# Experts in a written-out order on three engines: second product between the halves of the activation, slot work ahead, no weight splits on GpSimd

## Chip, cores, metric

One core of a Trainium2 chip runs the whole program. The metric is the device time of one execution in microseconds, as the median of several runs.

## What is computed

Two blocks act on 512 tokens of width 1024 in fp32. The first is a mixer (attention over selected keys beside a state-space branch), then a mixture of 32 experts with four experts a token; the second block is a gated mixer and a recurrent one. The change lies in the experts. Cut to them, the reference does this for every block of rows that one expert serves:

```python
def run_block(args):
    toks, e = args
    xb = h_pad[toks]
    gu = xb @ w_gu[e] + b_gu[e]
    g, u = gu[:, :D_EXPERT], gu[:, D_EXPERT:]
    g = jnp.minimum(g, SWIGLU_LIMIT)
    u = jnp.clip(u, -SWIGLU_LIMIT, SWIGLU_LIMIT)
    act = (u + 1.0) * (g * jax.nn.sigmoid(SWIGLU_ALPHA * g))
    return act @ w_dn[e] + b_dn[e]
...
out = out.reshape(n_rows, D) * row_gate[:, None].astype(out.dtype)
y = jax.ops.segment_sum(out, row_tok, num_segments=T + 1)[:T]
```

w_gu has 1024 x 2048 and w_dn 1024 x 1024 numbers an expert, 12 MiB together.

## The kernel before

The experts are ranked by how many tokens chose them. The first 17 ranks (NBIG) are *big*: they take up to 128 rows and compute in three matmuls of halves. A weight piece of 128 x 2048 numbers, 1 MiB, is *split* (split, L351) in two blocks of 1024 columns: ScalarE casts a block to H (L363), VectorE subtracts it from the raw piece and writes the rest to L (L365), and mm3 (L382 to L384) does the row halves against H, L and H. There are four H and four L buffers. The other 15 ranks are *small*: up to 64 rows, and the matmuls take the raw piece as it is.

The weights come by SP's queue in pieces of 1 MiB (wraw, L1690) into eleven buffers that are used in turn: eight pieces of w_gu and four of w_dn an expert. A load waits until the piece that had its buffer has been read: by the split for a big expert, by PE for a small one.

moe (from L1717 on) goes through the experts in the order TURNS. turns (L35) makes that list: three big ones first, then small and big in strict alternation, a small one last. In each turn it traces, in this order: the first product with w_gu (up, L1555, 96 matmuls and 4 for the bias; up64, L1571, 64 and 4); beside its pieces, one step a piece, the generator following, which fetches the expert after the next (one-hot L1542, slot product L1526 on PE, five or six small VectorE operations, gather on GpSimd's queue L1476); the transposes of the next expert's rows (transposed L1488, turned64 L1511); the first piece of the expert before's w_dn; the activation (glu, L1583); the rest of the expert before's second product (down L1629 and L382 to L384, 48 matmuls; down64 L1600 and L1606); the transposes of the activation (acted L1619, turned L1501). The scaled result goes out by a scatter that adds (L1645).

Traced order is not issue order. A scheduler sets each engine's order by priorities and readiness, and so a later product's matmuls can stand between two transposes. The second product that a turn traces is always that of the expert before.

glu (L1583 to L1593), for 512 columns at a time:

```python
nc.vector.tensor_scalar(g, gb, 7.0, None, op0=OP.min)
nc.scalar.activation(s, g, AF.Sigmoid, scale=1.702)
nc.vector.tensor_scalar(u, ub, 7.0, -7.0, op0=OP.min, op1=OP.max)
nc.gpsimd.tensor_tensor(s, s, g, op=OP.mult)
nc.vector.scalar_tensor_tensor(u, u, 1.0, s, op0=OP.add, op1=OP.mult)
```

A big expert runs it twice, a small one once. In a big expert's first product, GpSimd makes the first L block of pieces 1, 3 and 5 (pool=(1, 3, 5)), but not for the first expert in TURNS: 48 blocks.

inorder (L303) is there already and can chain VectorE's instructions in traced order; the expert stage does not use it.

Of the kernel before, what the change touches and what calls it, by code (L numbers as in the profile page):

```python
# [15 lines left out]
OP = mybir.AluOpType  # L16
AX = mybir.AxisListType

P = 128
D = 1024  # L20
S = 512
NT = 4
KD = 8
NE = 32
# [6 lines left out]
NBIG = 17  # L31
# [3 lines left out]
def turns():  # L35
    lead = max(1, 2 * NBIG - NE + 1)
    out, big = list(range(lead)), list(range(lead, NBIG))
    for r in range(NBIG, NE):
        out += [r] + big[:1]
        big = big[1:]  # L40
    return out
# [220 lines left out]
class Kern:  # L262
# [36 lines left out]
    @contextmanager  # L299
    def inorder(self, on=True):  # L300

        traced = self.nc.cur_bb.bb.instructions
        start = len(traced)  # L303
        yield
        last = None
        for i in traced[start:] if on else ():
            if i.engine == mybir.EngineType.DVE:
                if last is not None:
                    self.tc.add_manual_dep(i, last.name, mybir.DependencyInfo(mybir.DependencyClass.NoSync, mybir.DependencyReason.DATA), reason="in order")
                last = i  # L310

# [1206 lines left out]

    def slots(self, dst, oh, meta):

        nc = self.nc
        s0, n = dst
        b = self.bank()
        for e in range(n):
            for t in range(NT):
                nc.tensor.matmul(b[:, 4 * e:4 * e + 4], lhsT=oh[e][:, t], rhs=meta[:, t, s0 + e], start=t == 0, stop=t == NT - 1)  # L1526
        ms = self.small([P, n, 4])
        nc.vector.tensor_copy(ms, b[:, :4 * n].rearrange("p (e k) -> p e k", e=n))
        return self.slot_row(ms, n), ms
# [14 lines left out]

    def slot(self, r, oh, small=False):

        u, ms = self.slots((r, 1), [oh], self.meta)
# [36 lines left out]
    def glu(self, gb, ub):  # L1584

        nc = self.nc
        g, u, s = self.w2(), self.w2(), self.w2()
        nc.vector.tensor_scalar(g, gb, 7.0, None, op0=OP.min)  # L1588
        nc.scalar.activation(s, g, AF.Sigmoid, scale=1.702)  # L1589
        nc.vector.tensor_scalar(u, ub, 7.0, -7.0, op0=OP.min, op1=OP.max)  # L1590
        nc.gpsimd.tensor_tensor(s, s, g, op=OP.mult)  # L1591
        nc.vector.scalar_tensor_tensor(u, u, 1.0, s, op0=OP.add, op1=OP.mult)
        return u  # L1593

    def down64(self, x, sel, ws, gate, last=False):
# [11 lines left out]
        o = self.w4(shape=(P, 512)) if last else self.w2()  # L1607
        nc.vector.scalar_tensor_tensor(o, b, gate, self.gf2, op0=OP.mult, op1=OP.mult)
        return o

# [13 lines left out]
    def down(self, hl, sel, ws, gate, gf):  # L1624
# [11 lines left out]
        o = self.w4()  # L1636
        for n in range(2):
            sl = slice(n * 512, (n + 1) * 512)
            nc.vector.scalar_tensor_tensor(o[:, sl], bs[n], gate, gf[:, sl], op0=OP.mult, op1=OP.mult)
        return o  # L1640

# [86 lines left out]
    def moe(self):  # L1728
# [13 lines left out]
        def fetch(i):  # L1742

            r = TURNS[i]
# [5 lines left out]
            out[i] = self.gather(self.gidx[:64 if r >= NBIG else P, r:r + 1])  # L1750

        def following(i):
            if i == 0:
                self.route()
                yield
                self.slot(0, oh)
                fetch(1)
# [15 lines left out]
        prev = []  # L1773
        for i, r in enumerate(TURNS):
            small = r >= NBIG
            wg, wd = weights(i)
            if i:
                sel = (self.select64 if small else self.select)(self.eid[:, r:r + 1])
            self.bg = [following(i)]
            if small:  # L1780
                bs = self.up64(hl, sel, wg)
            else:
                with ExitStack() if i else self.tc.issue_after(self.first.ins):
                    bs = self.up(hl, sel, [(k, 0, lambda k=k: self.wraw(wg(k)), 2 * D) for k in range(KD)], (1, 3, 5) if i else ())
            if i == 0:
                self.rowload(self.gf, self.mrow[3], nc.gpsimd)
                for h in range(2):
                    row = self.mrow[3]
                    nc.gpsimd.dma_start(self.gf2[64 * h:64 * h + 64], bass.AP(tensor=row.tensor, offset=row.offset + 512 * h, ap=[[0, 64], [1, 512]]))
            self.drain()  # L1790
            if i + 1 < NE:
                hl = (self.turned64 if TURNS[i + 1] >= NBIG else self.transposed)(out.pop(i + 1))
            for step in prev[:1]:
                step()
            us = [self.glu(*bs)] if small else [self.glu(bs[n], bs[2 + n]) for n in range(2)]
            for step in prev[1:]:
                step()
            ah = self.turned(us[0]) if small else self.acted(us)

            def steps(r=r, small=small, ah=ah, sel=sel, wd=wd):  # L1800

                gate = self.gate[:, r:r + 1]
                got = {}

                def piece(kk):
                    if kk not in got:
                        w = self.wraw(wd(kk))
                        got[kk] = w if small else self.split(w)
                    return got.pop(kk)

                def begin():
                    got[0] = piece(0)

                def end():
                    o = self.down64(ah, sel, piece, gate, r == TURNS[-1]) if small else self.down(ah, sel, piece, gate, self.gf)
                    if r == TURNS[-1]:
                        return o
                    self.scatter(o, (self.sidx if small else self.gidx)[:, r:r + 1], small)
                return begin, end
            prev = steps()  # L1820
        o = prev[1]()
        row = self.t([P, 2048], "raw", 4)
# [32 lines left out]
    def overflow(self, gf):  # L1855
# [4 lines left out]
        with tc.For_i(0, n, 1) as i:  # L1860
# [49 lines left out]
            for t in range(NT):  # L1910
                nc.vector.tensor_scalar(oh[:, t], self.mcc("iota128"), col[:, t:t + 1], None, op0=OP.is_equal)
            u, ms = self.slots((0, 1), [oh], meta)
            gate = self.pt([P, 1], "ovg")
# [12 lines left out]
            bs = self.up(hl, sel, [(k, 0, lambda k=k: piece(wg[k * P:(k + 1) * P]), 2 * D) for k in range(KD)])  # L1926
            ah = self.acted([self.glu(bs[n], bs[2 + n]) for n in range(2)])
            o = self.down(ah, sel, lambda kk: self.split(piece(wd[kk * 256:(kk + 1) * 256].rearrange("(p k) n -> p (k n)", k=2))), gate, gf)
            for t, bs in enumerate(self.combine(u, o)):
# [367 lines left out]
```

## Time and profile before

| | |
|---|---|
| median of 3 runs | 2448.7 us (2447.04 to 2450.4) |
| the profiled execution's own time | 2447.35 us |
| its span, first to last instruction | 2445.6 us |
| mean granted clock of TensorE | 0.969 |
| PE busy | 2236.2 us (91%) |
| PE weight loads | 1591.1 us (65%) |
| VectorE | 1527.0 us (62%) |
| ScalarE | 988.5 us (40%) |
| GpSimd | 510.7 us (21%) |
| moved by DMA | 576.38 MB, mean 236 GB/s |

Busy times are shares of the whole span, over stages with different limits. Matmuls overlap, and PE counts as busy until the modelled end of one. A row of a timeline gives the start, the length, the line, the operation, out<-in, and in brackets how long the engine stood idle before it and what it waited for. at and mm are the two sets of four PSUM banks, H and L the split weights, hl the split rows, raw and XU the weight buffers, sx a small expert's turned rows.

### The profile page before, as it was taken

What the parts mean: (1) busy time and instruction counts of PE and PEld (TensorE: products, weight loads), DVE (VectorE), ACT (ScalarE), POOL (GpSimd) and SP (SyncE); (2) the same over time, 40 slices, a digit from 0 to 9 for tenths busy, and PEclk for the clock granted to TensorE, in tenths of its full rate; (3) what the DMA queues carried; (4) which work ended last, traced back from release to release, by engine and by line L of the source; (5) the groups of instructions that cost most, each with busy time, mean ns of one, the idle gap of its engine ahead of it and who ended that gap; (6) DMA issues with size and microseconds to landing.
All of it is one profiled execution on the core that took longest, in us unless ns stands there. A gap on an engine that the chain in (4) does not pass through costs nothing. (4 is left out here: it accounts for less than half of the span.)

```text
span 2445.6 us, 28109 instructions
## 1 busy us (share of the span) xinstructions
PE 2236.2 (91%) x10217; PEld 1591.1 (65%) x10217; DVE 1527.0 (62%) x2374; ACT 988.5 (40%) x1371; POOL 510.7 (21%) x274
## 2 busy tenths in 40 slices
PE   6999999998899889998889898889959999999898
PEld 4676666776776555565555565555537888888676
DVE  7778778765897555666655666655552443538864
ACT  4434443332664333344433344433323422326651
POOL 2011103322233222222222222221210111101210
PEclk9999999999999999999999999999979999999999
DMA  7233253644889999999999999999742222213220
GB/s 296 94 104 126 90 198 140 240 157 167 358 337 378 360 370 372 356 347 374 364 363 381 353 346 364 369 360 363 299 170 86 86 90 94 92 61 112 86 86 35
DMA packets 93940, 576.38 MB, mean 236 GB/s; under 512 B 12591, under 2 KB 14361, under 8 KB 32611
## 3 DMA queue, kind: packets, MB, share of 16 engines
q1 hardware_dynamic: 79856, 540.60, 58.1%
q0 software_dynamic: 8432, 18.21, 3.3%
q10 hardware_dynamic: 5508, 15.71, 1.8%
q8 instruction: 82, 1.34, 0.2%
q14 instruction: 62, 0.51, 0.1%
HBM read 556.74 MB, written 27.59 MB: 239 GB/s over the span
## 5 line engine op out<-in xcount | busy, mean ns | idle before, releaser
L365 DVE TENSOR_TENSOR L<-raw,H 128x1024 fp32r<-128x1024 f32 x439 | 613.4, 1430 | 264.5 <-ACT H L363 263.5
L363 ACT CAST H<-raw 128x1024 fp32r<-128x1024 f32 x501 | 515.8, 1048 | 410.0 <-PE mm L384 189.6
L365 POOL TENSOR_TENSOR L<-raw,H 128x1024 fp32r<-128x1024 f32 x62 | 167.6, 2705 | 514.7 <-ACT H L363 514.6
L383 PE MATMUL mm<-L,hl 128*128 128x512 f32 x544 | 217.4, 400 | 40.5 <-POOL L L365 23.1
L384 PE MATMUL mm<-H,hl 128*128 128x512 f32 x544 | 213.5, 393 | 0.0
L382 PE MATMUL mm<-U,H 128*128 128x512 f32 (+1 forms) x488 | 187.8, 385 | 3.0 <-DVE U L703 3.0
L383 PE MATMUL mm<-U,H 128*128 128x512 f32 (+1 forms) x488 | 186.8, 383 | 0.0
L384 PE MATMUL mm<-U,L 128*128 128x512 f32 (+1 forms) x488 | 186.0, 382 | 0.0
L1580 PE MATMUL mm<-raw,sx 128*64 128x512 f32 x792 | 177.5, 598 | 0.0
L382 PE MATMUL mm<-E,H 128*128 128x512 f32 x416 | 173.5, 419 | 3.7 <-ACT E L388 3.7
L382 PE MATMUL mm<-H,U 128*128 128x512 f32 x424 | 170.0, 401 | 2.6 <-DVE XU L2118 1.2
L382 PE MATMUL mm<-H,hl 128*128 128x512 f32 x544 | 170.4, 393 | 0.6 <-ACT hl L388 0.6
L383 PE MATMUL mm<-L,U 128*128 128x512 f32 x424 | 168.7, 398 | 0.0
L384 PE MATMUL mm<-H,U 128*128 128x512 f32 x424 | 168.4, 398 | 0.0
L383 PE MATMUL mm<-E,H 128*128 128x512 f32 x416 | 166.9, 401 | 1.5 <-DVE E L389 1.4
L384 PE MATMUL mm<-E,L 128*128 128x512 f32 x416 | 166.3, 400 | 0.0
L383 PEld LDWEIGHTS mm<-L,hl 128*128 128x128 f32 x544 | 102.1, 188 | 77.3 <-POOL L L365 30.2
L1591 POOL TENSOR_TENSOR w<-w,w 128x512 f32<-128x512 f32 x49 | 70.3, 1434 | 355.3 <-ACT w L1589 355.3
L1588 DVE TENSOR_SCALAR w<-mm 128x512 f32<-128x512 f32 x49 | 33.7, 687 | 171.8 <-PE mm L1580 152.2
L1589 ACT ACTIVATE w<-w 128x512 f32<-128x512 f32 x49 | 30.9, 631 | 262.5 <-DVE w L1588 262.4
L1580 PEld LDWEIGHTS mm<-raw,sx 128*64 128x64 f32 x792 | 54.9, 137 | 105.9 <-issue 102.8
L383 PE MATMUL at<-L,hl 128*128 128x512 f32 x272 | 118.6, 436 | 1.0 <-DVE L L365 1.0
(444 smaller groups left out, 4060.1 us busy)
## 6 DMA issues: line engine op xcount, KB each, us to landing
raw<-in_w_gu_dram SPq DMA_DIRECT2D x212, 1024.0 KB
raw<-in_w_dn_dram SPq DMA_DIRECT2D x103, 1024.0 KB
XU<-in_w_gu_dram SPq DMA_DIRECT2D x44, 1024.0 KB
XU<-in_w_dn_dram SPq DMA_DIRECT2D x25, 1024.0 KB
raw<-in_win_dram SPq DMA_DIRECT2D x20, 1024.0 KB
raw<-in_w_ada_dram SPq DMA_DIRECT2D x16, 1024.0 KB
raw<-in_wug_dram SPq DMA_DIRECT2D x16, 1024.0 KB
raw<-in_wxg_dram SPq DMA_DIRECT2D x12, 1024.0 KB
```

The lines of the kernel that those rows point to most:

```text
L363: nc.scalar.copy(h[:, :m], src)
L365: eng.tensor_tensor(l[:, :m], src, h[:, :m].bitcast(F32), op=OP.subtract)
L382: t.matmul(out, lhsT=lhs[0], rhs=rhs[0], start=start, stop=False)
L383: t.matmul(out, lhsT=lhs[0], rhs=rhs[1], start=False, stop=False)
L384: t.matmul(out, lhsT=lhs[1], rhs=rhs[0], start=False, stop=stop)
L1580: nc.tensor.matmul(bs[i // 2][64 * (i % 2):64 * (i % 2) + 64], lhsT=x[:, k], rhs=w[:, i * 512:(i + 1) * 512], start=False, stop=k == KD - 1)
L1588: nc.vector.tensor_scalar(g, gb, 7.0, None, op0=OP.min)
L1589: nc.scalar.activation(s, g, AF.Sigmoid, scale=1.702)
L1591: nc.gpsimd.tensor_tensor(s, s, g, op=OP.mult)
```

## The change

- TURNS: the first expert is big, then small and big alternate, and the 16 big ones are spread evenly over the 14 gaps between small ones, so that two gaps hold two.
- inorder takes a set of engines and keeps its last instruction over calls; from the second turn on, the instructions of PE, VectorE and ScalarE are chained in traced order.
- glu, down and down64 end early and hand back a function for their last VectorE operations. The turn calls them at set places: the activation's end (then) behind the split of the third w_dn piece of a big expert's second product, or ahead of a small one's; the second product's own end and its scatter (settle) behind the first split of the next big expert's first product, or ahead of a small expert's.
- A big expert's first two w_dn pieces (one in a big turn) are split ahead of the activation of the turn (begin).
- The selection matrix of the next expert is made at the end of a turn.
- fetch is a generator: one-hot, two steps later the slot product, a step later the slot's operations and the gather; in a small expert's turn the two next experts are fetched.
- GpSimd makes no weight split and no multiplication of the activation: pool=() and nc.vector in glu.

```diff
 def turns():
+    big, small = list(range(1, NBIG)), list(range(NBIG, NE))
+    gaps = max(1, len(small) - 1)
...
+    def inorder(self, on=True, engines=(mybir.EngineType.DVE,), last=None):
...
-    def up(self, hl, sel, pieces, pool=(1, 3, 5)):
+    def up(self, hl, sel, pieces, pool=(), then=None):
...
             w = self.split(w(), n, pool=k in pool)
+            if then and k == pieces[0][0]:
+                then()
...
-        nc.gpsimd.tensor_tensor(s, s, g, op=OP.mult)
-        nc.vector.scalar_tensor_tensor(u, u, 1.0, s, op0=OP.add, op1=OP.mult)
-        return u
+        def end():
+            nc.vector.tensor_tensor(s, s, g, op=OP.mult)
+            nc.vector.scalar_tensor_tensor(u, u, 1.0, s, op0=OP.add, op1=OP.mult)
+            return u
+        return end
...
             oh = self.w2(F32R, (P, NT, P))
             self.onehot(r, oh, small=r >= NBIG)
-            u = self.slot(r, oh, r >= NBIG)
+            yield
+            yield
+            b = self.counted([oh], self.meta, r, 1)
+            yield
+            u = self.slot(r, b, r >= NBIG)
...
-            if i + 2 < NE:
-                yield
-                fetch(i + 2)
-                yield
+            yield from fetch(i + 2)
+            if TURNS[i] >= NBIG:
+                yield from fetch(i + 3)
...
+                def ws(kk):
+                    w = d.got.pop(kk) if kk in d.got else d.piece(kk)
+                    if kk == 2 and not d.small:
+                        then()
+                    return w
...
+            with self.inorder(i > 0, (ET.PE, ET.DVE, ET.Activation), order):
+                if small:
+                    settle()
+                    bs = self.up64(hl, sel, wg)
+                else:
+                    with ExitStack() if i else self.tc.issue_after(self.first.ins):
+                        bs = self.up(hl, sel, [(k, 0, lambda k=k: self.wraw(wg(k)), 2 * D) for k in range(KD)], then=settle)
...
+                self.drain()
+                if down:
+                    down.begin(0 if down.small else 2 if small else 1)
+                glus = [self.glu(*bs)] if small else [self.glu(bs[n], bs[2 + n]) for n in range(2)]
+                if i + 1 < NE:
+                    hl = (self.turned64 if TURNS[i + 1] >= NBIG else self.transposed)(out.pop(i + 1))
+                us = []
+                then = lambda: us.extend(g() for g in glus)
+                if down:
+                    down.products(then)
+                    due.append(down.end)
+                else:
+                    then()
+                osel = sel
+                if i + 1 < NE:
+                    sel = selected(i + 1)
+                    if TURNS[i + 1] >= NBIG:
+                        settle()
+                ah = self.turned(us[0]) if small else self.acted(us)
+                down = Down(r, ah, osel, wd)
```

The overflow loop, which serves experts with more rows than they can hold, calls the split functions one after the other and computes as before.

How the instructions stand now is shown at two places. The first is PE at the end of a small expert's first product (the last L1580 rows; L1501 turns the small expert's activation, the L382 to L384 rows on at are the second product of the big expert before, L1526 a slot product). Before:

```order
L1580 MATMUL mm_7442<-raw_1667_7502,sx_7357 64x512 x2
L1580 MATMUL mm_7441<-raw_1668_7508,sx_7357 64x512 x2
L1580 MATMUL mm_7442<-raw_1668_7508,sx_7357 64x512 x2
L1501 MATMUL at_7636<-cst_66,w_1678_7540 128x128 x4
L382 MATMUL at_7547<-H_7531,hl_7416 128x512
L382 MATMUL at_7548<-H_7531,hl_7416 128x512
L1526 MATMUL at_7703<-meta_4966,w_1715_7701 128x4 x4
L383 MATMUL at_7547<-L_7532,hl_7416 128x512
L384 MATMUL at_7547<-H_7531,hl_7416 128x512
```

Now (line numbers have moved: L1590 is the first product, L1493 the transposes of the next expert's rows, L1645 and L387 to L389 the second product of the big expert before):

```order
L1590 MATMUL mm_8080<-raw_1814_8165,sx_8008 64x512 x2
L1590 MATMUL mm_8081<-raw_1814_8165,sx_8008 64x512 x2
L1493 MATMUL at_8198<-cst_66,w_1700_7663 128x128 x4
L1493 MATMUL at_8205<-cst_66,w_1700_7663 128x128 x4
L1645 MATMUL at_8212<-bias_4818,sel_7788 128x512
L1645 MATMUL at_8213<-bias_4818,sel_7788 128x512
L387 MATMUL at_8212<-H_8173,hl_8056 128x512
L388 MATMUL at_8212<-L_8174,hl_8056 128x512
L389 MATMUL at_8212<-H_8173,hl_8056 128x512
```

The activation's transposes, which stood right behind the first product, have given their place to the next expert's transposes and the second product; no slot product stands there.

The second place is the start of the next big expert's first product (its matmuls write mm). PE before:

```order
L384 MATMUL at_7547<-H_7613,hl_7416 128x512
L383 MATMUL at_7548<-L_7614,hl_7416 128x512
L384 MATMUL at_7548<-H_7613,hl_7416 128x512
L382 MATMUL mm_7653<-H_7659,hl_7514 128x512
L382 MATMUL mm_7654<-H_7659,hl_7514 128x512
L382 MATMUL mm_7655<-H_1708_7663,hl_7514 128x512
L382 MATMUL mm_7656<-H_1708_7663,hl_7514 128x512
```

And now:

```order
L387 MATMUL at_8213<-H_8270,hl_8056 128x512
L388 MATMUL at_8213<-L_8271,hl_8056 128x512
L389 MATMUL at_8213<-H_8270,hl_8056 128x512
L1506 MATMUL at_8289<-cst_66,w_1826_8192 128x128 x4
L387 MATMUL mm_8304<-H_8310,hl_8197 128x512
L388 MATMUL mm_8304<-L_8311,hl_8197 128x512
L389 MATMUL mm_8304<-H_8310,hl_8197 128x512
L387 MATMUL mm_8305<-H_8310,hl_8197 128x512
```

The four transposes of the small expert's activation (L1506) now stand between the last matmul of the second product and the first of the next big expert. ScalarE at the same place, where H_7659 and H_8310 are the first casts of the big expert; before:

```order
L1589 ACTIVATE w_1679_7541<-w_1677_7539 128x512
L363 CAST H_7531<-raw_1672_7529 128x1024
L363 CAST H_1675_7535<-raw_1672_7529 128x1024
L1502 COPY sx_7635<-at_7636 128x512
L363 CAST H_7565<-raw_1682_7563 128x1024
L363 CAST H_7569<-raw_1682_7563 128x1024
L1512 COPY sx_7855<-at_7856 128x512
L363 CAST H_7587<-raw_1687_7585 128x1024
L363 CAST H_1690_7591<-raw_1687_7585 128x1024
L363 CAST H_7609<-raw_7607 128x1024
L363 CAST H_7613<-raw_7607 128x1024
L363 CAST H_7659<-raw_7657 128x1024
```

Now:

```order
L368 CAST H_8183<-raw_8181 128x1024
L368 CAST H_8187<-raw_8181 128x1024
L1599 ACTIVATE w_1827_8193<-w_1825_8191 128x512
L393 CAST hl_8197<-at_8198 128x512
L393 CAST hl_8197<-at_8205 128x512
L368 CAST H_8242<-raw_8240 128x1024
L368 CAST H_1836_8246<-raw_8240 128x1024
L368 CAST H_8266<-raw_8264 128x1024
L368 CAST H_8270<-raw_8264 128x1024
L1507 COPY sx_8288<-at_8289 128x512
L368 CAST H_8310<-XU_8308 128x1024
```

The copy of the turned activation (sx, L1502 before, L1507 now) has moved from behind the second product's first two casts to behind its last, right ahead of the first cast of the big expert; two casts of w_dn now stand ahead of the sigmoid (the ACTIVATE row), where the sigmoid stood ahead of the first.

## Rows read from the trace of the kernel before

**Rows 1.** Windows: PE, PEld, DVE, ACT, POOL busy us (count), granted clock, DMA share, GB/s.

```profile
640.00:1760.00 1120.00, 1012.70 (x4512) 643.79 (x4510) 706.57 (x829) 479.34 (x535) 305.23 (x158) 0.97 0.96 363
820.00:830.00 10.00, 6.66 (x28) 4.71 (x25) 7.81 (x13) 4.99 (x6) 3.57 (x2) 0.83 1.01 425
1110.00:1130.00 20.00, 16.66 (x75) 12.72 (x72) 13.48 (x20) 12.86 (x15) 3.58 (x2) 0.91 1.01 418
```

**Rows 2.** Waits of weight loads (PEld) for a DMA, 640 to 1780: us, times, longest.

```profile
PEld at L1606 <- DMA raw<-in_w_gu_dram: 6.6, 20, 0.4
...
PEld mm L1580 <- DMA raw<-in_w_dn_dram: 2.8, 11, 0.3
```

**Rows 3.** Waits of PE from 640 to 1780 us: sum, times, longest.

```profile
PE at L1501 <- DVE w L1592: 45.7, 14, 3.3
PE mm L383 <- POOL L L365: 23.1, 16, 1.6
PE at L1526 <- DVE w L1542: 18.9, 13, 1.5
PE mm L383 <- DVE L L365: 17.2, 14, 1.3
```

**Rows 4.** Timeline of PE: start us, us, what; openings of three small experts.

```profile
1016.85 1.17 PE L1576 MATMUL mm<-bias,selz 128*128 128x512 f32 x4
...
1090.42 1.17 PE L1576 MATMUL mm<-bias,selz 128*128 128x512 f32 x4
...
1234.62 1.17 PE L1576 MATMUL mm<-bias,selz 128*128 128x512 f32 x4
```

**Rows 5.** Timeline of VectorE and GpSimd behind a small expert's first product.

```profile
1036.75 0.69 DVE L1588 TENSOR_SCALAR w<-mm 128x512 f32<-128x512 f32 x1 [10.06 <-PE mm L1580]
...
1038.24 1.78 POOL L1591 TENSOR_TENSOR w<-w,w 128x512 f32<-128x512 f32 x1 [14.20 <-ACT w L1589]
...
1040.06 0.69 DVE L1592 SCALAR_TENSOR_TENSOR w<-w,w 128x512 f32<-128x512 f32 x1 [1.16 <-POOL w L1591]
```

**Rows 6.** Timeline of PE behind the same product.

```profile
1040.90 1.09 PE L1501 MATMUL at<-cst,w 128*128 128x128 f32 x4 [3.34 <-DVE w L1592]
...
1043.92 0.63 PE L384 MATMUL at<-H,hl 128*128 128x512 f32 x1
1044.35 0.63 PE L383 MATMUL at<-L,hl 128*128 128x512 f32 x1
...
1049.49 0.39 PE L383 MATMUL at<-L,hl 128*128 128x512 f32 x1
1049.72 0.39 PE L384 MATMUL at<-H,hl 128*128 128x512 f32 x1
```

**Rows 7.** Window behind that hole (columns as in rows 1).

```profile
1040.90:1047.70 6.80, 6.80 (x20) 5.70 (x21) 5.07 (x9) 2.47 (x3) 1.79 (x1) 0.50 1.01 419
```

**Rows 8.** Low halves (L365): ns min/median/max, first and last; one stretch of VectorE.

```profile
L365 DVE TENSOR_TENSOR L<-raw,H x279: 1205/1218/4130, 640.8 to 1730.1; 128x1024 fp32r<-128x1024 f32 x140
L365 POOL TENSOR_TENSOR L<-raw,H x39: 2371/2931/3375, 661.4 to 1717.1; 128x1024 fp32r<-128x1024 f32 x39
...
1060.65 6.21 DVE L365 TENSOR_TENSOR L<-XU,H 128x1024 fp32r<-128x1024 f32 x3
```

**Rows 9.** Timeline of PE at a big expert's start.

```profile
1059.65 0.50 PE L383 MATMUL mm<-L,hl 128*128 128x512 f32 x1 [1.26 <-DVE L L365]
...
1063.55 0.50 PE L383 MATMUL mm<-L,hl 128*128 128x512 f32 x1 [1.57 <-POOL L L365]
```

**Rows 10.** ScalarE's copy of the turned activation and its casts: ns min/median/max.

```profile
L1502 ACT COPY sx<-at x14: 585/585/590, 763.9 to 1692.8; 128x512 f32<-128x512 f32 x14
...
L363 ACT CAST H<-raw x318: 1027/1049/1061, 640.3 to 1759.1; 128x1024 fp32r<-128x1024 f32 x159
```

**Rows 11.** DMA: the software queue's share of the span; the gathers' us to landing.

```profile
q0 software_dynamic: 8432, 18.21, 3.3%
...
w<-hd,gidx POOLq DMA_INDIRECT x31, 9.2
```

More of the change, by code (lines that the diff above doesn't have):

```diff
@@ L35, in turns @@
 def turns():
[L36 to L40, printed above, removed]
+    big, small = list(range(1, NBIG)), list(range(NBIG, NE))
+    gaps = max(1, len(small) - 1)
+    upto = lambda k: (2 * k * len(big) + gaps) // (2 * gaps)
+    more = [upto(k + 1) - upto(k) for k in range(gaps)]
+    out = [0]
+    for k, r in enumerate(small):
+        out.append(r)
+        if k < gaps:
+            out, big = out + big[:more[k]], big[more[k]:]
     return out
@@ L304, in inorder @@
         yield
-        last = None
+        last = {} if last is None else last
         for i in traced[start:] if on else ():
[L307 to L310, printed above, removed]
+            if i.engine in engines:
+                if i.engine in last:
+                    self.tc.add_manual_dep(i, last[i.engine].name, mybir.DependencyInfo(mybir.DependencyClass.NoSync, mybir.DependencyReason.DATA), reason="in order")
+                last[i.engine] = i
     def early(self, dt=F32, shape=(P, 4, 512)):
@@ L1543, in onehot, with slot @@
                                             pos[:, :, r:r + 1].to_broadcast([P, NT, P]), op=OP.is_equal)
-    def slot(self, r, oh, small=False):
-        u, ms = self.slots((r, 1), [oh], self.meta)
+    def slot(self, r, b, small=False):
+        u, ms = self.slots(b, 1)
         nc = self.nc
@@ L1606, in down64, with end @@
                     nc.tensor.matmul(b[64 * i:64 * i + 64], lhsT=x[:, j, 64 * h:64 * h + 64], rhs=w[:, k % 2 * D + i * 512:k % 2 * D + (i + 1) * 512], start=False, stop=k == KD - 1)
-        o = self.w4(shape=(P, 512)) if last else self.w2()
-        nc.vector.scalar_tensor_tensor(o, b, gate, self.gf2, op0=OP.mult, op1=OP.mult)
-        return o
+        def end():
+            o = self.w4(shape=(P, 512)) if last else self.w2()
+            nc.vector.scalar_tensor_tensor(o, b, gate, self.gf2, op0=OP.mult, op1=OP.mult)
+            return o
+        return end
     def acted(self, us):
@@ L1635, in down, with end @@
                     self.mm3(bs[n], (hl[:, 0, k * P:(k + 1) * P], hl[:, 1, k * P:(k + 1) * P]), w(j * D + n * 512, 512), False, k == KD - 1)
[L1636 to L1640, printed above, removed]
+        def end():
+            o = self.w4()
+            for n in range(2):
+                sl = slice(n * 512, (n + 1) * 512)
+                nc.vector.scalar_tensor_tensor(o[:, sl], bs[n], gate, gf[:, sl], op0=OP.mult, op1=OP.mult)
+            return o
+        return end
     def scatter(self, o, tok, small=False):
@@ L1742, in fetch @@
         def fetch(i):
+            if i >= NE or i in fetched:
+                return
+            fetched.add(i)
             r = TURNS[i]
@@ L1750, in fetch @@
             out[i] = self.gather(self.gidx[:64 if r >= NBIG else P, r:r + 1])
+        fetched = {0}
         def following(i):
@@ L1755, in following @@
                 yield
[L1756 to L1757 removed]
+                self.slot(0, self.counted([oh], self.meta, 0, 1))
+                yield from fetch(1)
                 yield
[L1759 to L1762 removed]
+            yield from fetch(i + 2)
+            if TURNS[i] >= NBIG:
+                yield from fetch(i + 3)
         def weights(i):
@@ L1771, in weights, with selected, __init__, piece @@
             return lambda k: g[k * P:(k + 1) * P], lambda kk: d[kk * 256:(kk + 1) * 256].rearrange("(p k) n -> p (k n)", k=2)
-        self.bg = []
-        prev = []
+        def selected(i):
+            r = TURNS[i]
+            return (self.select64 if r >= NBIG else self.select)(self.eid[:, r:r + 1])
+        class Down:
+            def __init__(d, r, ah, sel, wd):
+                d.r, d.ah, d.sel, d.wd, d.small, d.got = r, ah, sel, wd, r >= NBIG, {}
+            def piece(d, kk):
+                w = self.wraw(d.wd(kk))
+                return w if d.small else self.split(w)
+            def begin(d, n):
+                for kk in range(n):
+                    d.got[kk] = d.piece(kk)
+            def products(d, then):
+                gate = self.gate[:, d.r:d.r + 1]
+                def ws(kk):
[3 more added lines that the diff above has]
+                    return w
+                if d.small:
+                    then()
+                    d.finish = self.down64(d.ah, d.sel, ws, gate, d.r == TURNS[-1])
+                else:
+                    d.finish = self.down(d.ah, d.sel, ws, gate, self.gf)
+            def end(d):
+                self.scatter(d.finish(), (self.sidx if d.small else self.gidx)[:, d.r:d.r + 1], d.small)
+        self.bg = []
+        down, due, order = None, [], {}
+        ET = mybir.EngineType
+        def settle():
+            while due:
+                due.pop(0)()
         for i, r in enumerate(TURNS):
@@ L1776, in moe @@
             wg, wd = weights(i)
-            if i:
-                sel = (self.select64 if small else self.select)(self.eid[:, r:r + 1])
             self.bg = [following(i)]
[L1780 to L1819, printed above, removed]
@@ L1820, in moe @@
-            prev = steps()
-        o = prev[1]()
+            with self.inorder(i > 0, (ET.PE, ET.DVE, ET.Activation), order):
[5 more added lines that the diff above has]
+                        bs = self.up(hl, sel, [(k, 0, lambda k=k: self.wraw(wg(k)), 2 * D) for k in range(KD)], then=settle)
+                if i == 0:
+                    self.rowload(self.gf, self.mrow[3], nc.gpsimd)
+                    for h in range(2):
+                        row = self.mrow[3]
+                        nc.gpsimd.dma_start(self.gf2[64 * h:64 * h + 64], bass.AP(tensor=row.tensor, offset=row.offset + 512 * h, ap=[[0, 64], [1, 512]]))
+                self.drain()
[9 more added lines that the diff above has]
+                    due.append(down.end)
+                else:
+                    then()
+                osel = sel
[5 more added lines that the diff above has]
+                down = Down(r, ah, osel, wd)
@@ L1822, in moe @@
+        settle()
+        down.products(lambda: None)
+        o = down.finish()
         row = self.t([P, 2048], "raw", 4)
@@ L1926, in overflow @@
             bs = self.up(hl, sel, [(k, 0, lambda k=k: piece(wg[k * P:(k + 1) * P]), 2 * D) for k in range(KD)])
-            ah = self.acted([self.glu(bs[n], bs[2 + n]) for n in range(2)])
-            o = self.down(ah, sel, lambda kk: self.split(piece(wd[kk * 256:(kk + 1) * 256].rearrange("(p k) n -> p (k n)", k=2))), gate, gf)
+            ah = self.acted([self.glu(bs[n], bs[2 + n])() for n in range(2)])
+            o = self.down(ah, sel, lambda kk: self.split(piece(wd[kk * 256:(kk + 1) * 256].rearrange("(p k) n -> p (k n)", k=2))), gate, gf)()
             for t, bs in enumerate(self.combine(u, o)):
```

10 lines of the change are left out of this document (5 added, 5 removed).

## Prediction

> **What bounds the kernel now.** I read the views in this order: busy time by stretch, waits, one interval in order of time, the lengths of single operations. The page's slices put the DMA's full load into one stage, the experts, from 640 to 1760 us. There PE is busy 1012.7 of 1120 us, and the DMA is busy 96% of the time at 363 GB/s [rows 1]. So two candidates stand close together, and the reader has to see which of them ends the waits. PE hardly ever waits for a load: the two largest sums of weight loads held up by a DMA are 6.6 and 2.8 us, in pieces of at most 0.4 us [rows 2]. What PE waits for is computed [rows 3]: 14 times 3.3 us for the activation's product (45.7 us), 13 times 1.45 us for the one-hot of a slot (18.9 us), 23.1 and 17.2 us for low halves of a weight split. The loads for their part wait for buffers that these consumers hold. The stage is paced by PE and its chains, with the DMA not far behind.
>
> The pace is regular. The bias products that open a small expert start at 1016.85, 1090.42 and 1234.62 us [rows 4]: one interval of 73.6 us, then two of 72.1, mean 72.6. An interval holds one big and one small expert. Its largest hole follows the small expert's first product: clamp, sigmoid, GpSimd's multiplication of 1.78 us and a last VectorE operation come one after another [rows 5], and PE stands still for 3.34 us [rows 6]. [...] A stretch of 6.8 us at half speed loses 3.4 us, one of half that length 1.7; the 73.6 us interval holds the longer, the 72.1 us ones by their difference of 1.5 us the shorter, so the mean loss is 2.3 us.
>
> **The change part by part.** (a) The second product of the expert before now stands on PE right behind a small expert's first product, and the activation's end runs beside its third quarter. The 48 matmuls last 48 x 0.23 = 11.0 us; the chain that they hide lasted about 4 us. Saved: 3.3 us an interval, plus the clock's 2.3. If this cover went (the second product itself not ready), the 3.3 us would be back.
>
> (b) One-hots are made two pieces ahead of the four slot products, and both slots of a pair are fetched while a small expert runs. Saved: 1.45 us an interval. The slot work only moves within VectorE; it leaves the big expert's first product, where VectorE has the most to do.
>
> (c) The 48 weight splits and the activation's multiplications leave GpSimd. VectorE's split takes 1.218 us at the median, but up to 4.13 us; three beside a GpSimd split (2.93 us) took 6.21 us, 2.07 each [rows 8]. VectorE thus gets 48 x 1.22 = 59 us more splits and 49 multiplications, at the 0.69 us of its like operation [rows 5] 34 us. Against that stands its own contention: GpSimd's 48 splits take 48 x 2.93 = 141 us, at 2.07 a piece 68 of VectorE's run beside them and lose 0.85 each, 58 us. Net 35 us more, on an engine that is idle for 413 of 1120 us [rows 1]: I count nothing, and that idle time is the cover. In a big expert's first product VectorE then needs 16 x 1.22 = 19.5 us and 1.4 us for finishing the product before, PE 100 x 0.23 = 23 us: PE stays ahead as the slower. With every split at 2.07 us it would be 33 us; that is the upper bound of this part, and it lacks the GpSimd split that makes the 2.07.
>
> (d) What is late next is the start of a big expert's first product. Before, its first casts could run ahead of it; PE had 1.26 and 1.57 us of waiting there [rows 9], 40.3 us in all with 14 to 16 of each [rows 3], 2.8 an interval. Now ScalarE, in written order, makes the copy of the small expert's turned activation first. That copy needs four transposes that stand on PE behind the whole second product. Then come the cast and the low half: about 0.2 for the transposes' end, 0.59 and 1.05 [rows 10], 1.8 us until the first matmul, 1.22 - 0.23 = 1.0 until the second, and about 1.0 more when the two operations that finish the product before (0.7 us each) push back the third low half. New wait 3.9 us, 1.1 more than now. Whether the clock falls behind it no row shows: 1.26 and 1.57 with nine matmuls between them left it at 1.0, 3.34 in one piece did not. 2.9 us with one matmul in it lies nearer to the latter; I take half of 2.3, 1.2 us, between bounds of 0 and 2.3.
>
> (e) The order of experts: three big ones led, then strict alternation; now big and small alternate from the second on, and two pairs of big ones lie inside. The same 17 and 15 experts: nothing, give or take 5 us. In the first turn the second expert's gather is issued behind the fifth of eight pieces instead of the second; three pieces of 12 matmuls are left, 8.3 us, and a gather lands in 9.2 [rows 11]: a miss of 1 us or 2, once, inside those 5. SP's loads keep their order, weight blocks one after the other, and none passes another.
>
> **Sum.** 72.6 - 3.3 - 1.45 - 2.3 + 1.1 + 1.2 = 67.8 us, so 4.8 saved in each of 14 turns with a wait: 67 us. The DMA must still fit: an interval loads 24 MiB, 25.2 MB; stretches of 10 and 20 us run at 425 and 418 GB/s [rows 1], which makes 60 us. The software queue's gathers and scatters had 3.3% of the span [rows 11], 81 us for 32 experts, 5 an interval. 65 us fit into 67.8, but with little to spare, and eleven buffers, at 2.5 us a load, even out only 28 us; I take 10 us off for loads that come late. The gain is 57 us. The profiled execution took 2447.35 us, 1.3 under the median of 2448.7, so I forecast **2390 us**. With no more wait in (d) than before and no half-speed stretch, an interval takes 65.5 us, which the DMA's 65 just allow: 14 x 7.1 = 99, less the same 10, gives the low bound 2358. With the full 2.3 us of clock in (d), 5 us in (e) and 15 for late loads it is 14 x 3.7 - 20 = 32: 2415.
>
> [...]
>
> **The rivals.** *The DMA keeps its busy time.* If the 96% are true work, and the slow packets of the partly idle stretches stay slow when the loads come faster, only the 4% idle can go: 0.04 x 1120 = 45 us at best, half of it likely, 2425 us. For it: the mean of 363 against 418. Against it: the high rates appear just where several loads are queued, the low ones where each waits for a buffer.
>
> *No change.* The loads cannot do better than 363 GB/s on average, whatever PE does: 2447 us. [...] Against it stand the 20 us at 418.
>
> *Slower: written order behind a late load.* ScalarE and VectorE now make the splits of the next second product's first two pieces ahead of a small expert's clamp and sigmoid. If those pieces have not landed, the activation waits with them, and so does PE. Before, the sigmoid went first. Two pieces late are 2 x 2.5 us, then 2.3 us of cast and low half, and a half-speed stretch of 2.3: 9.6 us an interval. It decides from 4.8 us on, two loads late. I price it at 7 us, 2 above the gain: 14 x 2 = 28 us, 2475 us. For it: a small expert's first product takes 8 MiB in 15 us, faster than any rate above. Against it: today's loads are late by 0.4 us at most [rows 2], and eleven buffers run ahead.
>
> **How the numbers follow.** The forecast (2358 to 2415) has 0.62, the DMA that keeps its busy time (2402 to 2447) 0.20, no change 0.06, slower 0.12. A measurement tells about 0.2%, 4.9 us, from no change. Faster by more: 0.62 and nearly all of 0.20, 0.81. Within: 0.06 and the edge of the second case, 0.08. Slower: 0.11. The range that leaves out no more than 2 in 10 is 2358 to 2450.
>
> **What would show it.** Right: no PE wait behind the activation's last operation in the list of waits; none for a one-hot; every VectorE split near 1.22 us; intervals near 67 to 68 us; a new wait of 2 and 1 us at the big expert's first matmuls behind the turned copy; DMA rate above 380 GB/s over the stage. Wrong: intervals of 70 us with PE waiting for loads of weights (the DMA), unchanged intervals, or a sigmoid that starts late behind a cast that waited for a load.

## Result, and the profile after

The changed kernel takes 2369.18 us (median of 4 runs, 2367.14 to 2374.91) against 2449.55 us for the kernel before: a ratio of 0.9676, with an interval of 0.9657 to 0.9696. The profiled execution took 2369.02 us, 78.3 less than that of before; 57 were forecast.

| | before | after |
|---|---|---|
| span | 2445.6 us | 2366.8 us |
| PE busy | 2236.2 us | 2224.0 us |
| VectorE | 1527.0 us | 1523.1 us |
| GpSimd | 510.7 us | 309.1 us |
| mean granted clock | 0.969 | 0.972 |

No engine lost much busy time but GpSimd, which was never the busiest (PE lost 12 us). What went is idle time in the expert stage. Its windows answer to [rows 1]; the second is one interval (columns as there):

```profile
640.00:1690.00 1050.00, 1005.38 (x4522) 648.36 (x4523) 707.82 (x932) 479.10 (x539) 104.49 (x61) 0.98 0.98 388
1101.80:1168.10 66.30, 63.92 (x291) 40.60 (x290) 43.67 (x59) 29.27 (x33) 6.71 (x5) 0.97 0.99 395
```

The DMA moved 363 GB/s before, and moves 388 now, 395 in the interval. The openings of three small experts answer to [rows 4] (timeline of PE):

```profile
1033.06 1.17 PE L1586 MATMUL mm<-bias,selz 128*128 128x512 f32 x4
...
1100.65 1.17 PE L1586 MATMUL mm<-bias,selz 128*128 128x512 f32 x4
...
1232.59 1.17 PE L1586 MATMUL mm<-bias,selz 128*128 128x512 f32 x4
```

One interval of 67.6 us, then two of 66.0, mean 66.5: 6.1 less than before. The waits of PE over the stage answer to [rows 3]:

```profile
PE mm L387 <- ACT H L368: 25.9, 16, 1.6
PE mm L388 <- DVE L L370: 14.3, 20, 0.8
...
PE at L1516 <- DMA w<-hd,gidx: 2.0, 1, 2.0
```

The activation's 45.7 us, the one-hot's 18.9 and GpSimd's 23.1 are gone. In their place stands the wait that the prediction named, for the big expert's first cast (16 times 1.62 us) and its low half (16 times 0.76 us; the other four of the 20 are 0.53 us at its third low half). One gather was late, once, by 2.0 us. The same place in order of time, PE first and then ScalarE, answers to [rows 9, 10]:

```profile
1062.01 0.63 PE L1506 MATMUL at<-cst,w 128*128 128x128 f32 x4
1064.25 0.49 PE L387 MATMUL mm<-H,hl 128*128 128x512 f32 x1 [1.62 <-ACT H L368]
1065.51 0.80 PE L388 MATMUL mm<-L,hl 128*128 128x512 f32 x1 [0.76 <-DVE L L370]
...
1066.53 0.63 PE L387 MATMUL mm<-H,hl 128*128 128x512 f32 x1
1066.96 0.63 PE L388 MATMUL mm<-L,hl 128*128 128x512 f32 x1
```

```profile
1062.67 0.58 ACT L1507 COPY sx<-at 128x512 f32<-128x512 f32 x1 [5.01 <-PE at L1506]
1063.15 3.88 ACT L368 CAST H<-XU 128x1024 fp32r<-128x1024 f32 x4
```

The chain reads as forecast: transposes (L1506), the copy (sx), the cast (H), PE's first matmul after 1.62 us, its second 0.76 us later. Behind it matmuls start 0.43 us apart: the granted clock is 0.50 from 1066 to 1070 us. The half speed follows in 12 of the 16 starts. In the other four the same two waits leave the clock at 1.00, and there the third low half is waited for as well:

```profile
822.84 0.49 PE L387 MATMUL mm<-H,hl 128*128 128x512 f32 x1 [1.62 <-ACT H L368]
824.10 0.50 PE L388 MATMUL mm<-L,hl 128*128 128x512 f32 x1 [0.77 <-DVE L L370]
...
827.69 0.51 PE L388 MATMUL mm<-L,hl 128*128 128x512 f32 x1 [0.53 <-DVE L L370]
```

```profile
822.00:832.00 10.00, 7.86 (x32) 5.91 (x33) 9.18 (x9) 7.87 (x9) 2.34 (x1) 1.00 1.01 422
```

VectorE's splits (answering to [rows 8]) are now all alike, 1.211 to 1.228 us:

```profile
L370 DVE TENSOR_TENSOR L<-raw,H x322: 1211/1221/1228, 639.6 to 1679.5; 128x1024 fp32r<-128x1024 f32 x161
```

### The profile page after: what moved, and what is told of

Its sections match the earlier page's. It is cut to its first block, busy times and chain, and to the rows that moved or that the text cites. A ratio compares the mean times of both kernels' runs of the same rounds, so it can differ in the third digit from the quotient of the medians.

```text
span 2366.8 us, 28018 instructions
## 1 busy us (share of the span) xinstructions
PE 2224.0 (94%) x10217; PEld 1592.0 (67%) x10217; DVE 1523.1 (64%) x2471; ACT 984.9 (42%) x1371; POOL 309.1 (13%) x177
## 5 line engine op out<-in xcount | busy, mean ns | idle before, releaser
L370 DVE TENSOR_TENSOR L<-raw,H 128x1024 fp32r<-128x1024 f32 x478 | 590.1, 1259 | 286.1 <-ACT H L368 277.3
L387 PE MATMUL mm<-H,hl 128*128 128x512 f32 x544 | 223.4, 411 | 25.9 <-ACT H L368 25.9
L388 PE MATMUL mm<-L,hl 128*128 128x512 f32 x544 | 225.0, 414 | 14.3 <-DVE L L370 14.3
L389 PE MATMUL mm<-H,hl 128*128 128x512 f32 x544 | 222.2, 408 | 0.0
L387 PE MATMUL mm<-U,H 128*128 128x512 f32 (+1 forms) x488 | 187.6, 384 | 3.0 <-DVE U L708 3.0
L389 PE MATMUL mm<-U,L 128*128 128x512 f32 (+1 forms) x488 | 185.7, 382 | 0.0
L1590 PE MATMUL mm<-raw,sx 128*64 128x512 f32 x792 | 180.3, 598 | 0.0
L387 PE MATMUL mm<-E,H 128*128 128x512 f32 x416 | 173.6, 420 | 3.7 <-ACT E L393 3.7
L387 PE MATMUL mm<-H,U 128*128 128x512 f32 x424 | 170.0, 401 | 2.3 <-DVE w L2256 1.1
L389 PE MATMUL mm<-H,U 128*128 128x512 f32 x424 | 168.2, 397 | 0.4 <-DVE U L394 0.4
L389 PE MATMUL mm<-E,L 128*128 128x512 f32 x416 | 166.3, 400 | 0.0
L387 PEld LDWEIGHTS mm<-H,hl 128*128 128x128 f32 x544 | 107.0, 197 | 53.0 <-ACT H L368 29.0
L388 PEld LDWEIGHTS mm<-L,hl 128*128 128x128 f32 x544 | 107.5, 198 | 45.6 <-DVE L L370 21.0
L389 PEld LDWEIGHTS mm<-H,hl 128*128 128x128 f32 x544 | 107.7, 198 | 23.7
L1590 PEld LDWEIGHTS mm<-raw,sx 128*64 128x64 f32 x792 | 54.1, 137 | 98.6 <-issue 94.5
L370 POOL TENSOR_TENSOR L<-raw,H 128x1024 fp32r<-128x1024 f32 x23 | 55.2, 2401 | 444.5 <-ACT H L368 444.5
L388 PE MATMUL at<-L,hl 128*128 128x512 f32 x272 | 108.2, 398 | 2.3 <-DVE L L370 2.3
```

The lines of the kernel that those rows point to most:

```text
L370: eng.tensor_tensor(l[:, :m], src, h[:, :m].bitcast(F32), op=OP.subtract)
L387: t.matmul(out, lhsT=lhs[0], rhs=rhs[0], start=start, stop=False)
L388: t.matmul(out, lhsT=lhs[0], rhs=rhs[1], start=False, stop=False)
L389: t.matmul(out, lhsT=lhs[1], rhs=rhs[0], start=False, stop=stop)
L1590: nc.tensor.matmul(bs[i // 2][64 * (i % 2):64 * (i % 2) + 64], lhsT=x[:, k], rhs=w[:, i * 512:(i + 1) * 512], start=False, stop=k == KD - 1)
```

## Experiments

Every kernel was timed beside the kernel before (2449 us in all). e1 to e4 and e12 each take one part of the change back.

**The activation's end and its transposes ahead of the second product (e1).**

```diff
                 then = lambda: us.extend(g() for g in glus)
+                if small:
+                    then()
+                    ah = self.turned(us[0])
+                    then = lambda: None
                 if down:
...
-                ah = self.turned(us[0]) if small else self.acted(us)
+                ah = ah if small else self.acted(us)
```

> The changed kernel, but a small expert's activation ends, and is transposed, ahead of the big expert's second product, as before; the multiplication stays on VectorE. Theory (PE paces the stage, and what counts is the sum of its waits): the wait of 2.4 us at the big expert's start goes, since the copy is early; behind the small expert's first product comes a chain of about 2.8 us, 1.1 of it covered by the next expert's transposes, so a wait of 1.7 to 2.0. Within 10 us of 2369, in either direction. Rival (hiding the chain is the gain by itself): 14 times 3.3 us and the half speed behind it come back, 2369 + 45 to 75.

Measured: 2411.92 us, ratio 0.9842 (0.9826 to 0.9859), 43 us above the changed kernel. My figure for it fell; the rival's lower end is close. The waits of PE name the place:

```profile
PE at L1506 <- DVE w L1604: 74.4, 15, 5.4
```

It is 5.3 us a turn, not 2. I had added up the chain and not what a written order puts into it and ahead of it. PE's end of the first product, then VectorE in order of time:

```profile
1063.45 3.65 PE L1590 MATMUL mm<-raw,sx 128*64 128x512 f32 x16
...
1073.44 1.10 PE L1506 MATMUL at<-cst,w 128*128 128x128 f32 x4 [5.31 <-DVE w L1604]
```

```profile
1064.28 4.62 DVE L370 TENSOR_TENSOR L<-raw,H 128x1024 fp32r<-128x1024 f32 x4
1068.82 0.68 DVE L1598 TENSOR_SCALAR w<-mm 128x512 f32<-128x512 f32 x1
1069.42 0.68 DVE L1600 TENSOR_SCALAR w<-mm 128x512 f32<-128x512 f32 x1
1070.67 1.29 DVE L394 TENSOR_TENSOR hl<-at,hl 128x512 fp32r<-128x512 f32 x2 [0.57 <-ACT hl L393]
1071.88 0.68 DVE L1603 TENSOR_TENSOR w<-w,w 128x512 f32<-128x512 f32 x1
1072.60 0.69 DVE L1604 SCALAR_TENSOR_TENSOR w<-w,w 128x512 f32<-128x512 f32 x1
```

Two things add some 1.7 us each. The four splits of the next second product's first two pieces (L370) stand ahead of the clamp, which starts 1.7 us after the product's end at 1067.1. And the two low halves of the next expert's rows (L394) stand between clamp and multiplication, and they wait for ScalarE. So the chain costs more in a written order than the 3.3 us that it cost before, when the scheduler let it through; e1 prices that hole, and not the former one.

**GpSimd's splits back (e2), its multiplication back (e12).**

```diff
-    ... for k in range(KD)], then=settle)
+    ... for k in range(KD)], (1, 3, 5) if i else (), then=settle)
```

```diff
-            nc.vector.tensor_tensor(s, s, g, op=OP.mult)
+            nc.gpsimd.tensor_tensor(s, s, g, op=OP.mult)
```

> The changed kernel with the 48 GpSimd splits back (pieces 1, 3 and 5 of each big expert's first product but the first's). Theory (they contend with VectorE's splits and are slower than these): VectorE's splits beside them take 2.1 us and more again, PE waits for low halves, 1 to 2 us in each of 16 first products: 2369 + 15 to 35. Rival (they were a help to VectorE, or hidden): 2369, or up to 10 less.

> The changed kernel with the activation's multiplication back on GpSimd. Theory (the second product hides the chain with room to spare): within 5 us of 2369. Rival (written order: VectorE's low halves of the third and fourth piece stand behind the activation's last operation and now wait 1.1 us longer): 2369 + 10 to 25.

Measured: 2366.92 us (ratio 0.9660, 0.9643 to 0.9678) and 2365.71 us (0.9659, 0.9644 to 0.9674). Neither can be told from the changed kernel. VectorE's splits grow longer in e2 (2.76 us at most, against 1.23 in the changed kernel), and it costs nothing:

```profile
L370 DVE TENSOR_TENSOR L<-raw,H x287: 1209/1218/2762, 639.1 to 1689.4; 128x1024 fp32r<-128x1024 f32 x144
...
L370 POOL TENSOR_TENSOR L<-raw,H x38: 2393/2602/2947, 699.4 to 1642.6; 128x1024 fp32r<-128x1024 f32 x38
```

```profile
PE mm L388 <- POOL L L370: 2.1, 6, 0.4
```

PE waits for GpSimd 2.1 us in all. My theory for e2 fell, e12's held. In the written order neither edit is a part of the gain by itself; the two together were not run.

**The same edit to the kernel before (e7).** There it does something:

```diff
-    ... for k in range(KD)], (1, 3, 5) if i else ())
+    ... for k in range(KD)], ())
```

> The kernel before with one edit: no split on GpSimd. Theory (contention): the low halves come sooner, the 23 us of waits for GpSimd's go and the 17 us for VectorE's shrink: 2449 - 15 to 40. Rival (VectorE gets 59 us more work and is late with it): 2449 + 0 to 15.

Measured: 2434.0 us, ratio 0.9932 (0.9912 to 0.9953), 15.5 us less, at a lower mean granted clock (0.961 in the profiled execution, 0.969 before). PE's waits are those of [rows 3] without GpSimd's 23.1 us:

```profile
PE at L1501 <- DVE w L1592: 45.7, 14, 3.3
PE at L1526 <- DVE w L1542: 18.9, 13, 1.5
PE mm L383 <- DVE L L365: 17.3, 14, 1.3
```

At a big expert's start the second of the two waits ([rows 9], 1.57 us) was for a GpSimd split. In the changed kernel PE stands there anyway, for the copy, and the same lateness seems to hide behind that: e2 has the 25.9 us for the first cast unchanged and 2.1 us for GpSimd. Part costs do not add up.

**The former order of experts (e3), and the new one alone in the kernel before (e8).** turns() is exchanged for that of the other kernel, nothing else.

> The changed kernel with the former order of experts, three big ones first and then strict alternation. Theory: the same work with the same waits, within 6 us of 2369. Rival (spreading the big ones keeps the loads ahead and was part of the gain): 2369 + 15 or more.

> The kernel before with one edit: the new order of experts. Theory: within 6 us of 2449. Rival (spreading the big ones matters by itself): 2449 - 10 or more.

Measured: 2364.22 us (ratio 0.9645, 0.9627 to 0.9663), 5 us below the changed kernel with intervals that just overlap, and 2456.58 us (1.0022, 1.0011 to 1.0033), 7 us above the kernel before. Both point the same way: in a stage that PE paces, the new order gives nothing and may cost some 5 us.

**Slots at once (e4).**

```diff
...
             self.onehot(r, oh, small=r >= NBIG)
-            yield
-            yield
             b = self.counted([oh], self.meta, r, 1)
-            yield
             u = self.slot(r, b, r >= NBIG)
...
-            yield from fetch(i + 2)
-            if TURNS[i] >= NBIG:
-                yield from fetch(i + 3)
+            yield
+            fetch(i + 2)
+            yield
```

> The changed kernel with the one-hot, the slot product and its operations traced together in one step, one expert a turn, as before. Theory: in a written order PE meets the slot product 1.45 us too early in each turn, and VectorE's slot operations stand in the middle of the big expert's splits: 31 times about 1.4 us, 2369 + 20 to 45. Rival (PE's one-hot wait was slack that the loads would have taken anyway): 2369 + 0 to 8.

Measured: 2406.3 us, ratio 0.9821 (0.9803 to 0.9839): 37 us more, inside the theory's range. Of its two reasons only the second shows: PE has no wait for a one-hot or at the slot product. Its longest sum is now low halves that come late, 42.6 us where the changed kernel has 14.3:

```profile
PE mm L388 <- DVE L L370: 42.6, 40, 1.8
```

VectorE stands still in the middle of the splits until PE's slot product is done, 2.23 us in the interval looked at, and PE then waits 1.69 us for the next low half.

**No written order (e5).**

```diff
-            with self.inorder(i > 0, (ET.PE, ET.DVE, ET.Activation), order):
+            with self.inorder(False):
```

> The changed kernel as traced, but no engine's instructions are chained: the scheduler sets the order again. Theory (the written order is what keeps the second product between the halves of the activation): the scheduler moves the activation's end and its transposes forward again, and a good part of the 80 us is lost, 2369 + 20 to 60. Rival (tracing the parts in this order is enough): 2369, give or take 8.

Measured: 2409.84 us, ratio 0.9836 (0.9815 to 0.9857): 41 us more. Both removed waits are back, that for the activation shorter, 2.21 us a turn instead of 3.34:

```profile
PE at L1506 <- DVE w L1604: 30.9, 14, 2.2
PE at L1530 <- DVE w L1550: 19.0, 13, 1.5
```

```profile
1049.50 8.75 PE L1590 MATMUL mm<-raw,sx 128*64 128x512 f32 x40
1060.46 0.60 PE L1506 MATMUL at<-cst,w 128*128 128x128 f32 x3 [2.21 <-DVE w L1604]
```

```profile
1058.91 0.68 DVE L1603 TENSOR_TENSOR w<-w,w 128x512 f32<-128x512 f32 x1
```

The transposes (L1506) stand right behind the first product again: tracing the parts in the new order hides neither wait, the chaining of the three engines does, and it is worth 41 us. The 39 us that stay without it do not come from the traced order alone. The waits that are less than before are mostly those that GpSimd caused: its splits' 23.1 us are gone (15.5 us of time in e7), and the activation's are 14.8 us shorter, 1.13 a turn, where its multiplication takes 0.68 us instead of GpSimd's 1.78. So leaving GpSimd alone does count as long as the scheduler sets the order, and no longer in the written one. No run separates these 39 us further.

**The new wait taken away (e6).** The small expert's transposes and copy move ahead of the last quarter of the second product.

```diff
                     if kk == 2 and not d.small:
                         then()
+                    if kk == 3 and not d.small:
+                        late()
...
+                turned = []
+                late = (lambda: turned.append(self.turned(us[0]))) if small else (lambda: None)
                 if down:
-                    down.products(then)
+                    down.products(then, late)
...
-                ah = self.turned(us[0]) if small else self.acted(us)
+                ah = (turned or [self.turned(us[0])])[0] if small else self.acted(us)
```

> The changed kernel with the small expert's four transposes and the copy moved ahead of the last quarter of the second product, so that the next big expert's first cast no longer waits for them. Theory (PE still paces the stage): most of the 2.4 us wait goes, and with it the half speed, 14 times 2 to 4 us: 2369 - 28 to 50. Rival (the loads are now the bound, at 24 loads and the gathers in 65 us against intervals of 66): the interval cannot fall by more than 1.2 us, 2369 - 0 to 17, and PE shows waits for loads instead.

Measured: 2340.96 us, ratio 0.9561 (0.9537 to 0.9584): 28 us below the changed kernel, the best version of the study. That is the theory's low end. The wait is gone but for the two big experts that follow a big one, and most of the half speed with it: the granted clock stood at half for 51 us of the stage (640 to 1700 us) in the changed kernel and for 14 here.

```profile
PE mm L387 <- ACT H L368: 3.3, 2, 1.6
```

Whether more was held back by the loads the next run tells.

**How far the loads let it go (e10).** This kernel leaves out the product of the rows' high halves with the weights' low halves in the expert stage, from the second expert on.

```diff
...
-        t.matmul(out, lhsT=lhs[0], rhs=rhs[1], start=False, stop=False)
+        if not self.lean:
+            t.matmul(out, lhsT=lhs[0], rhs=rhs[1], start=False, stop=False)
...
+            self.lean = i > 0
...
```

> The changed kernel without one of the three matmuls of each weight half in the expert stage from the second expert on (the rows' high half times the weights' low half is left out, a third of every big expert's products; all loads, splits, gathers and scatters stay). PE has 11 us less an interval. Theory (the changed kernel is still paced by PE at 66 us, the loads need 65): the interval falls to the loads' 62 to 65 us, 2369 - 15 to 60, with PE waiting for splits of late loads. Rival 1 (the loads are far from their limit): 2369 - 120 to 160. Rival 2 (the loads already pace the changed kernel): 2369 - 0 to 8.

Measured: 2343.71 us, ratio 0.9566 (0.9552 to 0.9581): 25 us less than the changed kernel, and not less than e6, with 11 us less of matmuls an interval. By these two runs that is the floor of the loads. From 800 to 1600 us, e10 first, then e6 with an early window beside it:

```profile
800.00:1600.00 800.00, 678.14 (x2889) 373.07 (x2888) 548.25 (x726) 374.27 (x426) 70.52 (x47) 0.97 1.01 400
```

```profile
680.00:760.00 80.00, 78.95 (x363) 52.52 (x362) 59.93 (x75) 41.81 (x47) 9.12 (x5) 1.00 1.00 403
800.00:1600.00 800.00, 775.59 (x3542) 501.04 (x3539) 560.51 (x731) 379.78 (x429) 74.56 (x47) 0.99 1.00 399
```

The DMA is busy all the time and moves 400 and 399 GB/s; PE is idle for 122 of 800 us in e10. ScalarE's casts show what they wait for, in e10 and, less, in the changed kernel:

```profile
ACT H L369 <- DMA raw<-in_w_dn_dram: 220.5, 24, 22.4
```

```profile
ACT H L368 <- DMA raw<-in_w_dn_dram: 27.0, 18, 3.6
```

The changed kernel thus stands some 25 us above the loads' floor and is still paced by PE; e6 has reached the floor.

**Two variants of e6 (e9 with the former order of experts, e11 with the sigmoid ahead of one of the two casts' pieces).** e9 exchanges turns() again; the edit shown is e11's, on top of e6.

```diff
-                    down.begin(0 if down.small else 2 if small else 1)
+                    down.begin(0 if down.small else 1)
                 glus = [self.glu(*bs)] if small else [self.glu(bs[n], bs[2 + n]) for n in range(2)]
+                if down and small and not down.small:
+                    down.got[1] = down.piece(1)
```

> e6_transposes_inside with the former order of experts, three big ones first. Theory (the order of experts cost e3 nothing and the changed kernel perhaps 5 us): 2341 - 0 to 8. Rival (e6 is bound by the loads, and a lead of three big experts lets the loads fall behind or run ahead differently): 2341 + 5 or more.

> e6_transposes_inside with only one of the two w_dn pieces split ahead of the small expert's clamp and sigmoid, the other behind them. Theory (in e6 the loads are the bound, so what the sigmoid waits for behind a late piece costs nothing of its own): within 6 us of 2341. Rival (the written order behind a late load costs e6 time): 2341 - 8 or more.

Measured: 2360.34 us (0.9630, 0.9617 to 0.9643) and 2343.17 us (0.9559, 0.9545 to 0.9574). e11 is e6 again: where the loads pace, it costs nothing here that the sigmoid stands behind a cast that waits for one. e9 is 19 us slower than e6, so here the order of experts does matter. The early window shows how:

```profile
680.00:760.00 80.00, 73.88 (x341) 51.78 (x340) 62.85 (x83) 42.17 (x48) 7.05 (x5) 1.00 0.85 311
800.00:1600.00 800.00, 773.55 (x3516) 481.44 (x3512) 526.25 (x702) 350.90 (x398) 75.05 (x49) 0.99 1.01 400
```

While three big experts follow each other, the loads get only 311 GB/s; e6 has 403 there. 92 GB/s over 80 us are 7.4 MB, 18 us at the 400 GB/s that both hold later. A likely reason is that big experts free buffers slowly: the loads' queue waits 44.0 us of these 80 for low halves in e9, 34.4 in e6. No run shows that by itself.

## Why the prediction was right

**The bound.** It was PE and its chains, as read; the DMA lay close behind, 25 us away at the end (e10). "The DMA keeps its busy time" and "no change" did not come: the same bytes took less busy time, 395 GB/s in the interval at a share of 0.99, where 363 stood at 0.96; why is not shown. The 363 GB/s of the stage before were no bound of the loads: e10 and e6 hold 400 and 399 for 800 us.

**(a) and (b), the removed waits.** Both are gone to the last row, and they come back with 41 us when the chaining goes (e5). e1 and e4 cost 43 and 37 us, but neither brings its former wait back: e1 has a hole of 5.3 us and loses the new wait of (d), e4 has late low halves in place of the wait for the one-hot. They are no prices of (a) and (b), and they do not add up to the gain.

**(c), GpSimd.** Counted at nothing; e2 and e12 confirm it for the changed kernel. e7 shows that its 15.5 us exist in the kernel before; in my sum they sat in the 2.8 us of the big expert's start. The working was off: VectorE was to be 35 us busier and is 4 us less busy (1527.0 before, 1523.1 after), so without GpSimd it got back about 97 us by the same sum (an estimate), not 58.

**(d), the new wait.** The mechanism is the right one, and its size was off: 25.9 and 14.3 us over 16 starts are 2.5 us, not 3.9. The first two items measured 1.62 and 0.76 us against 1.8 and 1.0. The third, the low half pushed back by the end of the product before, is 0.53 us against 1.0 in the four starts that keep the clock at 1.00, and hides in the other twelve, where the matmuls ahead of it run at a clock of 0.50. That is 1.4 us, 14 times, 19 us. The half speed that I gave a half chance is nearly always there. The granted clock stood at half for 61 us of the stage before (640 to 1770 us), a loss of 2.2 us in each of 14 turns against the sum's 2.3, which is worked out from [rows 4, 7]; it stood at half for 51 after, so it gave back 5 us where the sum has 14 x (2.3 - 1.2) = 15: 10 us on the other side.

**(e)** was priced at nothing, give or take 5: e3 and e8 say 5 to 7 us against. The gather's miss of "1 us or 2, once" was 2.0.

**The sum.** The term that failed besides (d) is the 10 us for late loads: it was not needed, as the changed kernel runs above the loads' floor. 57 + 19 + 10 - 5 for the order of experts - 10 for the clock make 71 against 78 measured. That the number fell inside the range is in part luck: terms were wrong on both sides. The rest of 7 lies where the sum had no term. From 626.8 us, where the kernels still run alike, to the first matmul behind the last expert, PE is also busy 10.8 us less with the same work, of which the clock is 5; why is not shown:

```profile
626.80:1797.50 1170.70, 1046.50 (x4663) 667.46 (x4661) 731.88 (x879) 495.99 (x554) 307.35 (x159) 0.97 0.94 355
626.80:1720.10 1093.30, 1035.69 (x4666) 669.11 (x4664) 729.16 (x976) 492.36 (x554) 106.04 (x62) 0.97 0.96 380
```

**Slower behind a late load.** The mechanism exists: in e10 the casts wait 220.5 us for loads. It decides nothing in the changed kernel, whose casts wait 27.0 us and where PE waits for no load of weights, nor in e6, where putting the sigmoid ahead changes nothing (e11).

## What to carry to other kernels

When a chain between two products is hidden by moving a third one into it, look at what now stands between that product and the next: here the copy that ended the chain had become the next late thing, and moving it one quarter earlier gave another 28 us. A written order has to be checked operation by operation on each engine, since it also holds back what a scheduler had let through (e1). Taking parts back one by one does not price them: GpSimd's edits count without the chaining (e5, e7) and not with it (e2, e12). Before counting on more, measure the loads' floor by leaving out compute and keeping the transfers: it tells when to stop, and from then on the order of experts counts too (e9).

## Not expected

A GpSimd split that costs 15.5 us in one order of instructions costs nothing in another (e7, e2), though VectorE's splits beside it are slow there too (up to 2.76 us, before up to 4.13). Two idle stretches of PE of 1.62 and 0.76 us with one matmul between them were followed by a granted clock of 0.50 in 12 of 16 starts of a big expert and not in the other four; 1.26 and 1.57 us with nine matmuls between them were not in the interval shown ahead (clock 1.00 from 1059 to 1066 us).
